# Gate units spread between the attentions of a two-layer encoder, and two softmax scalings moved to ScalarE

## The chip, the core and the metric

The kernel runs on one core of a Trainium2 chip. The metric is the device time of one execution in microseconds (us). Engines are named as in the profile: PE is TensorE, PEld its weight loads, DVE is VectorE, ACT is ScalarE, POOL is GpSimd, SP is SyncE, which here only issues transfers.

## What is computed

Two layers. Each normalises x (512 tokens of 1024), projects it to eight groups of columns, runs two kinds of attention, multiplies each by a gate, and adds an output projection to x. All data are float32.

```python
h = rmsnorm(x, norm_g[l])
proj = h @ w_in[l]                       # q_a k_a v_a g_a | q_b k_b v_b g_b
out_a = neighborhood_attention(q_a, k_a, v_a, na_rpb[l])      # group A: 8 heads of 64
out_b = diff_attention(q_b, k_b, v_b, t5_table, lam, ...)     # group B: 4 heads, two softmax maps each
y = concatenate([out_a * silu(g_a), out_b * silu(g_b)])
x = x + y @ w_out[l]
# group B: attn = softmax(map 0) - lam * softmax(map 1), then attn @ v, then an RMS norm per head
```

## The kernel before

The input projection is cut into 16 units per layer of 256 columns of w_in: `VB0 VB1` and `VA0 VA1` (values of group B and A), `QB0..QB3` and `QA0..QA3` (queries and keys of one B head, or of one pair of A heads), `GB0 GB1` and `GA0 GA1` (gates). Between them stand eight attentions, `AB0..AB3` (one B head each) and `AA0..AA3` (a pair of A heads each; below, x and y are the first and second head of a pair). The tuple `ORDER` says in which order a layer's units and attentions are written.

Every matmul is done three times for precision: each operand is split into a rounded part and the rest (`wh`, `wl`; `hTh`, `hTl`; `pth`, `ptl`). ACT makes the rounded part (line L98 for weights, L163 for results), DVE subtracts it (L101, L164). A Q or G unit is 48 matmuls of 512 columns at L210, a V unit 96 of 256 columns at L222; both write a PSUM tile `pp`, of which there are three. The output projection is L540; it starts with the halves of `y` that belong to group B.

A quarter of a B head (128 queries) is: scores on PE (L271, L272, into `st`, two buffers), DVE adds the bias and takes the minimum (L274), ACT exponentiates (L277), this for both maps; DVE takes reciprocals (L281, L282), scales the first map (L283) and subtracts the second (L284); PE transposes (L288, into `pt`, two buffers), ACT and DVE split the result (L163, L164); PE multiplies by the values (L293, into `pv`, one buffer). After a head come squares, a sum over partitions on PE (L304), DVE's `row` (L306) and on POOL three small transfers, a power (L308 to L314) and a product (L315). A quarter of an A head ("tile") is the same with 256 columns and one map: L325, L331, L334, reciprocal L336, scale L337, transposes L340, split L163/L164; after four tiles the products L347 and their sum (L353 on ACT, L354 on DVE).

A gate is evacuated by a tanh on ACT (L252) and a product on DVE (`u`, L254); POOL multiplies it into `y` (L483). `u` shares its two buffers with `rb`, which holds the norm factors of a B head.

Weights are converted two units ahead: when a unit begins, the L98 and L101 of the unit after next are written, into the buffer pair of the unit that has just begun, so they wait until PE has done with it. The program is written in `ORDER`; a list scheduler then decides, from estimates of its own, in which order each engine's queue takes the instructions. Each engine then works through its queue in that order.

Of the kernel before, what the change touches and what calls it, by code (L numbers as in the profile page):

```python
# [11 lines left out]
AF = mybir.ActivationFunctionType  # L12
# [16 lines left out]
WARM = (7, 2)  # L29
WRAW_BUFS = 2  # L30
QK_BUFS = 2
ORDER = ("VB0", "QB0", "AB0", "QB1", "VB1", "AB1", "QB2", "AB2", "QB3", "AB3", "VA0", "QA0", "AA0",
         "QA1", "AA1", "VA1", "QA2", "AA2", "QA3", "AA3", "GB0", "GB1", "GA0", "GA1")
A_TILES = ((0, 1), (1, 1), (2, 1), (0, 3))
A_SLOT = ((0, 0, 256), (1, 1, 128), (2, 1, 128), (0, 1, 768))
A_PV = ((1, 0, 128), (3, 256, 128), (0, 0, 384), (2, 128, 128))
# [5 lines left out]
def _view(t, off, dims):  # L42
    return bass.AP(tensor=t.tensor, offset=t.offset + off, ap=[list(t.ap[0])] + [list(d) for d in dims])
# [3 lines left out]
def hybrid_encoder(ctx: ExitStack, tc: tile.TileContext, x, norm_g, w_in, na_rpb,  # L47
# [18 lines left out]
    V, A, G, T = nc.vector, nc.scalar, nc.gpsimd, nc.tensor  # L66
# [95 lines left out]
    def split(ps, oh, ol):  # L162
        A.copy(out=oh, in_=ps)  # L163
        V.tensor_tensor(out=ol, in0=ps, in1=oh.bitcast(F32), op=ALU.subtract)  # L164
# [93 lines left out]
    def attn_b(h, q, k, vt, yb, nlam, sg, yout):  # L258
        pv = ps_v.tile([P, S], F32, name="pv")
        for qp in range(2):  # L260
            pth_v = w4.tile([P, 4, 256], F32R, name="pth", tag="w4k")
            ptl_v = w4.tile([P, 4, 256], F32R, name="ptl", tag="w4k")
            for qi in range(2):
                qt = 2 * qp + qi
                e = w4.tile([P, 2, S], F32, name="w4k")
                mn = small.tile([P, 2], F32, name="mn")
                z = small.tile([P, 2], F32, name="z")
                for m in range(2):
                    st = ps_s.tile([P, S], F32, name="st")
                    kh, kl = k[m]  # L270
                    T.matmul(out=st, lhsT=q[m][:, qt * P:(qt + 1) * P], rhs=kh, start=True, stop=False)  # L271
                    T.matmul(out=st, lhsT=q[m][:, qt * P:(qt + 1) * P], rhs=kl, start=False, stop=True)  # L272
                    lt = work.tile([P, S], F32, name="lt", bufs=2)
                    V.tensor_tensor_reduce(out=lt, in0=st, in1=yb[:, 48 - 16 * qt:560 - 16 * qt],  # L274
                                           scale=-1.0, scalar=3e38, op0=ALU.add, op1=ALU.min,
                                           accum_out=mn[:, m:m + 1])
                    A.activation(out=e[:, m, :].rearrange("p (b r c) -> p b r c", r=ROWS, c=C8),  # L277
                                 in_=lt.rearrange("p (r b c) -> p b r c", r=ROWS, c=C8),
                                 func=AF.Exp, bias=mn[:, m:m + 1], scale=-1.0, accum_out=z[:, m:m + 1])
                rz = small.tile([P, 2], F32, name="rz")  # L280
                V.reciprocal(out=rz, in_=z)  # L281
                V.tensor_scalar_mul(rz[:, 1:2], rz[:, 1:2], nlam)  # L282
                V.tensor_scalar_mul(e[:, 0, :], e[:, 0, :], rz[:, 0:1])  # L283
                V.scalar_tensor_tensor(out=e[:, 0, :], in0=e[:, 1, :], scalar=rz[:, 1:2], in1=e[:, 0, :],  # L284
                                       op0=ALU.mult, op1=ALU.add)
                pt = ps_t.tile([P, 4, P], F32, name="pt")
                for kt in range(4):
                    T.transpose(out=pt[:, kt, :], in_=e[:, 0, kt * P:(kt + 1) * P], identity=ident)  # L288
                split(pt, pth_v[:, :, qi * P:(qi + 1) * P], ptl_v[:, :, qi * P:(qi + 1) * P])
            n = 0  # L290
            for kt in range(4):
                for vs, pp in ((0, pth_v), (0, ptl_v), (1, pth_v)):
                    T.matmul(out=pv[:, qp * 256:(qp + 1) * 256], lhsT=vt[:, kt, h % 2, vs, :], rhs=pp[:, kt, :],  # L293
                             start=(n == 0), stop=(n == 11))
                    n += 1
        sq, su = (work.tile([64, S], F32, name=nm, tag="s2", bufs=3) for nm in ("sq", "su"))
        A.activation(out=sq, in_=pv[0:64], func=AF.Square)
        A.activation(out=su, in_=pv[64:P], func=AF.Square)
        V.tensor_tensor(out=sq, in0=sq, in1=su, op=ALU.add)
        A.activation(out=yout, in_=pv, func=AF.Copy, scale=sg)  # L300
        sr = work.tile([P, S], F32R, name="sr", tag="s2", bufs=3)
        A.copy(out=sr[0:64], in_=sq)
        V.tensor_tensor(out=sr[64:P], in0=sq, in1=sr[0:64].bitcast(F32), op=ALU.subtract)
        T.matmul(out=pv[0:2, :], lhsT=ones_r, rhs=sr, start=True, stop=True)  # L304
        row = work.tile([1, S], F32, name="row", tag="th", bufs=2)
        V.tensor_scalar(out=row, in0=pv[0:1, :], scalar1=1.0 / P, scalar2=1e-5, op0=ALU.mult, op1=ALU.add)  # L306
        ms = small.tile([P, 4], F32, name="ms")
        nc.gpsimd.dma_start(out=ms, in_=row.rearrange("o (p a) -> o p a", a=4))  # L308
        rs = small.tile([P, 4], F32, name="rsb")
        G.tensor_tensor(out=rs, in0=ms, in1=nhalf, op=ALU.pow)  # L310
        rs_d = dram.tile([1, S], F32, name="rs_d", bufs=2)
        nc.gpsimd.dma_start(out=rs_d.rearrange("o (p a) -> (o p) a", a=4), in_=rs)
        rb = work.tile([P, S], F32, name="rb", tag="u", bufs=2)
        nc.gpsimd.dma_start(out=rb, in_=rs_d.broadcast_to([P, S]))  # L314
        G.tensor_tensor(out=yout, in0=yout, in1=rb, op=ALU.mult)  # L315


    def attn_a(l, hd, half, q, k, vt, s_out):
        ba = bias_a(l, hd)
        ptt = [w4.tile([P, 4, 256], F32R, name=nm, tag="w4k") for nm in ("pth", "ptl")]  # L320
        z = small.tile([P, 4], F32, name="za")
        for j, (k0, dk) in enumerate(A_TILES):
            st = ps_s.tile([P, S], F32, name="st")
            for i in range(2):
                T.matmul(out=st[:, 0:256], lhsT=q[:, j * P:(j + 1) * P],  # L325
                         rhs=k[i].rearrange("p (t c) -> p t c", c=P)[:, k0:k0 + dk + 1:dk, :],
                         start=(i == 0), stop=(i == 1))
            e = work.tile([P, 256], F32, name="ea", bufs=3)
            mn = small.tile([P, 1], F32, name="mna")
            i0 = (0, 4, 4, 8)[j]  # L330
            V.tensor_tensor_reduce(out=e, in0=st[:, 0:256],  # L331
                                   in1=ba[:, 64 * i0:64 * i0 + 256],
                                   scale=-1.0, scalar=3e38, op0=ALU.add, op1=ALU.min, accum_out=mn)
            A.activation(out=e, in_=e, func=AF.Exp, bias=mn, scale=-1.0, accum_out=z[:, j:j + 1])  # L334
            rz = small.tile([P, 1], F32, name="rza")
            V.reciprocal(out=rz, in_=z[:, j:j + 1])  # L336
            V.tensor_scalar_mul(e, e, rz)  # L337
            pt = ps_t.tile([P, 4, P], F32, name="pt")
            for i in range(2):
                T.transpose(out=pt[:, i, :], in_=e[:, i * P:(i + 1) * P], identity=ident)  # L340
            t0, sl, stp = A_SLOT[j]
            oh, ol = (_view(p, t0 * 256 + sl * P, [[stp, 2], [1, P]]) for p in ptt)
            split(pt[:, 0:2, :], oh, ol)
        pv = ps_v.tile([P, S], F32, name="pv")
        for n, (t, q0, dq) in enumerate(A_PV):
            for i, pp in enumerate(ptt):
                T.matmul(out=_view(pv, q0, [[dq, 2], [1, P]]), lhsT=vt[:, t, hd % 4, :],  # L347
                         rhs=pp[:, t, :].rearrange("p (a b) -> p a b", b=P),
                         start=(n == 0 and i == 0), stop=(n == 3 and i == 1))
        tmp = work.tile([P, S], F32, name="tmpa", tag="s2", bufs=3)  # L350
        lo = 64 * half
        hi = 64 - lo
        A.activation(out=tmp[lo:lo + 64], in_=pv[hi:hi + 64], func=AF.Copy, scale=0.5)  # L353
        V.scalar_tensor_tensor(out=s_out[lo:lo + 64], in0=pv[lo:lo + 64], scalar=0.5, in1=tmp[lo:lo + 64],  # L354
                               op0=ALU.mult, op1=ALU.add)
# [3 lines left out]
    for l in range(DEPTH):  # L359
        seq += [(w_in[l, UNITS.index(u)], False) for u in ORDER if u in UNITS]  # L360
        seq += [(w_out[l, i], i == 3) for i in range(4)]
# [95 lines left out]
    for l in range(DEPTH):  # L457
# [38 lines left out]
        nlam, sg = lams[l]  # L496
        for n, u in enumerate(ORDER):
            kind, i = u[:2], int(u[2])
# [182 lines left out]
```

## Time and profile before

| | |
|---|---|
| median of 3 runs | 631.58 us (631.32 to 632.37) |
| the profiled execution | 631.53 us |
| its span, first to last instruction | 629.8 us |
| PE busy | 594.4 us, 94% of the span |
| DVE busy | 427.0 us, 68% |
| ACT busy | 320.2 us, 51% |
| mean granted TensorE clock | 0.977 |

The 1.7 us between time and span are outside the first and last instruction. A busy PE may still be slow: matmuls are pipelined and the table counts an engine as busy from start to modelled end. Layer 1 and 2 repeat each other with 303.4 us between them; the rows below are mostly of layer 1.

### The profile page before, as it was taken

What the parts mean: (1) busy time and instruction counts of PE and PEld (TensorE: products, weight loads), DVE (VectorE), ACT (ScalarE), POOL (GpSimd) and SP (SyncE); (2) the same over time, 40 slices, a digit from 0 to 9 for tenths busy, and PEclk for the clock granted to TensorE, in tenths of its full rate; (3) what the DMA queues carried; (4) which work ended last, traced back from release to release, by engine and by line L of the source; (5) the groups of instructions that cost most, each with busy time, mean ns of one, the idle gap of its engine ahead of it and who ended that gap; (6) DMA issues with size and microseconds to landing.
All of it is one profiled execution on the core that took longest, in us unless ns stands there. A gap on an engine that the chain in (4) does not pass through costs nothing.

```text
span 629.8 us, 9006 instructions
## 1 busy us (share of the span) xinstructions
PE 594.4 (94%) x3230; PEld 504.5 (80%) x3230; DVE 427.0 (68%) x1011; ACT 320.2 (51%) x672; POOL 73.6 (12%) x91
## 2 busy tenths in 40 slices
PE   9899995899989999999999999688998999999995
PEld 7888883788888888888898798577887888888883
DVE  2755667597887777754674576578788877777263
ACT  5433546374656555734254344635666556664232
POOL 4400000111022002200000000020101200111001
PEclk9999997989999999999999999979999999999998
DMA  6854232313533443453643533320335354226214
GB/s 233 150 187 119 86 101 85 102 47 104 139 93 117 126 137 120 137 176 132 202 134 100 163 91 99 103 68 1 85 100 143 106 154 125 93 68 206 95 67 134
DMA packets 25166, 74.48 MB, mean 118 GB/s; under 512 B 7329, under 2 KB 7329, under 8 KB 24098
## 3 DMA queue, kind: packets, MB, share of 16 engines
q1 hardware_dynamic: 23648, 71.51, 37.6%
q0 software_dynamic: 1472, 2.40, 2.3%
q8 instruction: 26, 0.43, 0.3%
q14 instruction: 18, 0.15, 0.1%
q10 hardware_dynamic: 2, 0.00, 0.0%
HBM read 60.23 MB, written 4.21 MB: 102 GB/s over the span
## 4 chain that ended last, share of the span: by engine, by line
PE 81%; DVE 10%; ACT 5%; issue 3%; POOL 0%; POOLq 0%; DVEq 0%; ACTq 0%
PE pp L210 39%; PE pp L540 11%; PE pp L222 11%; PE pv L293 3%; PE pv L347 2%; PE pt L340 2%; DVE lt L274 2%; DVE wl L101 2%; PE st L325 2%; PE st L271 2%; PE pv L540 2%; PE st L272 2%; PE pt L288 1%; PE pt L195 1%; PE pp L437 1%
## 5 line engine op out<-in xcount | busy, mean ns | idle before, releaser
L101 DVE TENSOR_TENSOR wl<-wraw,wh 128x512 fp32r<-128x512 f32 x148 | 93.5, 686 | 52.6 <-ACT wh L98 20.7
L98 ACT CAST wh<-wraw 128x1024 fp32r<-128x1024 f32 x74 | 74.3, 1048 | 67.4 <-PE pp L210 33.8
L210 PE MATMUL pp<-hTh,wl 128*128 128x512 f32 x384 | 106.1, 399 | 0.0
L210 PE MATMUL pp<-hTh,wh 128*128 128x512 f32 x384 | 102.3, 398 | 0.4 <-DVE kt L246 0.4
L210 PE MATMUL pp<-hTl,wh 128*128 128x512 f32 x384 | 102.6, 396 | 0.0
L210 PEld LDWEIGHTS pp<-hTl,wh 128*128 128x128 f32 x384 | 70.7, 188 | 14.9
L210 PEld LDWEIGHTS pp<-hTh,wh 128*128 128x128 f32 x384 | 69.7, 188 | 14.6 <-PE pt L288 0.9
L210 PEld LDWEIGHTS pp<-hTh,wl 128*128 128x128 f32 x384 | 70.1, 188 | 14.0
L163 ACT CAST pth<-pt 128x256 fp32r<-128x256 f32 (+1 forms) x96 | 42.3, 443 | 70.2 <-PE pt L288 47.5
L222 PE MATMUL pp<-wh,hTh 128*128 128x256 f32 x224 | 66.0, 295 | 7.4 <-DVE v L164 7.0
L164 DVE TENSOR_TENSOR ptl<-pt,pth 128x256 fp32r<-128x256 f32 (+1 forms) x96 | 48.6, 508 | 31.3 <-ACT pth L163 30.6
L222 PE MATMUL pp<-wh,hTl 128*128 128x256 f32 x224 | 65.4, 292 | 0.0
L222 PE MATMUL pp<-wl,hTh 128*128 128x256 f32 x224 | 65.1, 290 | 0.0
L222 PEld LDWEIGHTS pp<-wh,hTh 128*128 128x128 f32 x224 | 44.2, 197 | 10.4 <-DVE v L164 7.9
L277 ACT ACTIVATE w4k<-lt,mn 128x512 f32<-128x512 f32 x64 | 45.9, 721 | 5.4 <-DVE mn L274 5.1
L274 DVE CUSTOM_DVE_ANT_0 lt<-st,yb 128x512 f32<-128x512 f32 x64 | 43.1, 681 | 3.4 <-PE st L272 2.9
L331 DVE CUSTOM_DVE_ANT_0 ea<-st,ba 128x256 f32<-128x256 f32 x64 | 26.4, 419 | 27.3 <-PE pt L340 19.6
L222 PEld LDWEIGHTS pp<-wl,hTh 128*128 128x128 f32 x224 | 44.0, 196 | 0.6
L222 PEld LDWEIGHTS pp<-wh,hTl 128*128 128x128 f32 x224 | 43.9, 196 | 0.5
L271 PE MATMUL st<-kt,qs 128*128 128x512 f32 x64 | 29.1, 454 | 11.0 <-DVE mn L274 9.2
L483 POOL TENSOR_TENSOR y<-y,u 128x512 f32<-128x512 f32 x16 | 21.6, 1348 | 144.7 <-DVE u L254 122.2
L334 ACT ACTIVATE ea<-ea,mna 128x256 f32<-128x256 f32 x64 | 32.7, 513 | 9.7 <-DVE mna L331 8.2
(124 smaller groups left out, 1066.7 us busy)
## 6 DMA issues: line engine op xcount, KB each, us to landing
wraw<-in_w_in_dram SPq DMA_DIRECT2D x64, 512.0 KB, 4.0
kt<-kt SPq DMA_DIRECT2D x16, 512.0 KB, 4.4
wraw<-in_w_out_dram SPq DMA_DIRECT2D x16, 512.0 KB, 3.7
ba<-in_na_rpb_dram SPq DMA_DIRECT2D x16, 384.0 KB, 3.6
y<-in_x_dram SPq DMA_DIRECT2D x8, 512.0 KB, 4.5
yb<-in_t_table_dram SPq DMA_DIRECT2D x8, 280.0 KB, 2.8
rb<-rs_d POOLq DMA_DIRECT2D x8, 256.0 KB, 4.4
xs_d<-y SPq DMA_DIRECT2D x4, 512.0 KB, 4.3
```

The source lines that it names most:

```text
L98: A.copy(out=wh[:, ks, :], in_=r)
L101: V.tensor_tensor(out=wl[:, kh, :], in0=r[:, 2 * i:2 * i + 2, :], in1=wh[:, kh, :].bitcast(F32), op=ALU.subtract)
L163: A.copy(out=oh, in_=ps)
L164: V.tensor_tensor(out=ol, in0=ps, in1=oh.bitcast(F32), op=ALU.subtract)
L210: T.matmul(out=pp, lhsT=a[:, kc, cs], rhs=b[:, kc, c0:c0 + S], start=(n == 0), stop=(n == 3 * KC - 1))
L222: T.matmul(out=pp[:, 0:256], lhsT=a[kc][:, c0:c0 + P], rhs=b[:, kc, :], start=(n == 0), stop=(n == 3 * KC - 1))
L271: T.matmul(out=st, lhsT=q[m][:, qt * P:(qt + 1) * P], rhs=kh, start=True, stop=False)
L274: V.tensor_tensor_reduce(out=lt, in0=st, in1=yb[:, 48 - 16 * qt:560 - 16 * qt], scale=-1.0, scalar=3e38, op0=ALU.add, op1=ALU.min, accum_o ...
L277: A.activation(out=e[:, m, :].rearrange("p (b r c) -> p b r c", r=ROWS, c=C8), in_=lt.rearrange("p (r b c) -> p b r c", r=ROWS, c=C8), fun ...
L331: V.tensor_tensor_reduce(out=e, in0=st[:, 0:256], in1=ba[:, 64 * i0:64 * i0 + 256], scale=-1.0, scalar=3e38, op0=ALU.add, op1=ALU.min, acc ...
L334: A.activation(out=e, in_=e, func=AF.Exp, bias=mn, scale=-1.0, accum_out=z[:, j:j + 1])
L540: T.matmul(out=pp, lhsT=a[k][:, t * P:(t + 1) * P], rhs=b[:, kc, :], start=(half + kc + i == 0), stop=(half == 1 and kc == 3 and i == 2))
```

## The change

`ORDER` gets a new sequence. GB0 goes from the end of the layer to the place between QB2 and AB2, GB1 to the place before AA0, GA0 to the place before AA3; GA1 stays last. VA0 is written one attention earlier. The scaling of the first map (L283) and of group A's exponentials (L337) is written as an ACTIVATE with a per-partition scale instead of a DVE multiplication.

```diff
-ORDER = ("VB0", "QB0", "AB0", "QB1", "VB1", "AB1", "QB2", "AB2", "QB3", "AB3", "VA0", "QA0", "AA0",
-         "QA1", "AA1", "VA1", "QA2", "AA2", "QA3", "AA3", "GB0", "GB1", "GA0", "GA1")
+ORDER = ("VB0", "QB0", "AB0", "QB1", "VB1", "AB1", "QB2", "GB0", "AB2", "QB3", "VA0", "AB3", "QA0", "GB1",
+         "AA0", "QA1", "VA1", "AA1", "QA2", "AA2", "QA3", "GA0", "AA3", "GA1")
...
-                V.tensor_scalar_mul(e[:, 0, :], e[:, 0, :], rz[:, 0:1])
+                A.activation(out=e[:, 0, :], in_=e[:, 0, :], func=AF.Copy, scale=rz[:, 0:1])
...
-            V.tensor_scalar_mul(e, e, rz)
+            A.activation(out=e, in_=e, func=AF.Copy, scale=rz)
```

How the change stands in the queues, at the three places that the prediction speaks of. First DVE in layer 1 during AB1, where the last products of AB0 come in. Before, the four L101 rows convert the weights of QA0 and wait for QB3:

```order
L164 TENSOR_TENSOR ptl<-pt,pth 128x4x128
L101 TENSOR_TENSOR wl<-wraw,wh 128x512 x4
L299 TENSOR_TENSOR sq<-sq,su 64x512
L164 TENSOR_TENSOR ptl<-pt,pth 128x4x128
L274 ISA lt,mn<-st,yb 128x512
```

After the change they convert the weights of VA0 and wait for GB0, which now stands where QB3 stood:

```order
L299 TENSOR_TENSOR sq<-sq,su 64x512
L101 TENSOR_TENSOR wl<-wraw,wh 128x512 x4
L164 TENSOR_TENSOR ptl<-pt,pth 128x4x128
L303 TENSOR_TENSOR sr<-sq,sr 64x512
L274 ISA lt,mn<-st,yb 128x512
```

The four conversions stay ahead of the minimum (L274) in both; the sum of squares (L299) has moved ahead of them. Second, ACT at the start of AA0, from the evacuation of QA1's first query half (the first L231) to that of its second. Before, the values of VA1 (`v`) are evacuated between the steps of AA0:

```order
L231 ACTIVATE qs<-pp 64x512
L334 ACTIVATE ea,za<-ea,mna 128x256
L163 CAST pth<-pt 128x4x128
L163 CAST pth<-pt 128x2x128
L334 ACTIVATE ea,za<-ea,mna 128x256
L297 ACTIVATE sq<-pv 64x512
L298 ACTIVATE su<-pv 64x512
L300 ACTIVATE y<-pv,sg_366 128x512
L163 CAST v<-pp 128x4x64
L163 CAST pth<-pt 128x256
L163 CAST v<-pp 128x4x64
```

And after the change, up to just ahead of the second L231:

```order
L334 ACTIVATE ea,za<-ea,mna 128x256
L297 ACTIVATE sq<-pv 64x512
L298 ACTIVATE su<-pv 64x512
L300 ACTIVATE y<-pv,sg_366 128x512
L163 CAST pth<-pt 128x2x128
L337 ACTIVATE ea<-ea,rza 128x256
L163 CAST pth<-pt 128x256
L334 ACTIVATE ea,za<-ea,mna 128x256 x2
L302 CAST sr<-sq 64x512
L163 CAST pth<-pt 128x256
L334 ACTIVATE ea,za<-ea,mna 128x256
L337 ACTIVATE ea<-ea,rza 128x256 x2
```

The evacuations of `v` are gone from here, because VA1 comes later, and the scalings have come in. Third, PE at the end of the layer. Before, the last tiles of AA3 (L340) lie between the matmuls of the last gate unit, GA1 (L210), up to the output projection:

```order
L340 MATMUL pt<-ident,ea 128x128 x2
L210 MATMUL pp<-hTh,wh 128x512 x3
L210 MATMUL pp<-hTl,wh 128x512 x8
L210 MATMUL pp<-hTh,wl 128x512 x4
L347 MATMUL pv<-pth,v 128x256
L210 MATMUL pp<-hTh,wl 128x512
L347 MATMUL pv<-ptl,v 128x256
L210 MATMUL pp<-hTh,wl 128x512
L340 MATMUL pt<-ident,ea 128x128 x2
L210 MATMUL pp<-hTh,wl 128x512 x2
L540 MATMUL pp<-wh,yTh 128x512
```

After the change the last matmuls of GA1 are followed by most of AA3. First the rows just behind GA1:

```order
L210 MATMUL pp<-hTh,wl 128x512 x3
L347 MATMUL pv<-pth,v 128x256
L325 MATMUL st<-kt,qs 128x256 x2
L347 MATMUL pv<-ptl,v 128x256
L347 MATMUL pv<-pth,v 128x2x128
L347 MATMUL pv<-ptl,v 128x2x128
L347 MATMUL pv<-pth,v 128x256
L347 MATMUL pv<-ptl,v 128x256
L340 MATMUL pt<-ident,ea 128x128 x2
L325 MATMUL st<-kt,qs 128x256 x2
L340 MATMUL pt<-ident,ea 128x128 x2
L325 MATMUL st<-kt,qs 128x256 x2
```

From GA1's last matmul to the first L540 there stand four pairs of scores, six pairs of transposes and 14 products of values in PE's queue, and no matmul of a projection.

## Rows read from the trace of the kernel before

**Rows 1.** The page: span, and busy time by engine.
```profile
span 629.8 us, 9006 instructions
PE 594.4 (94%) x3230; PEld 504.5 (80%) x3230; DVE 427.0 (68%) x1011; ACT 320.2 (51%) x672; POOL 73.6 (12%) x91
```

**Rows 2.** Stretches: length, busy time (instructions) of each engine, clock, DMA share, GB/s.
```profile
90.00:135.00 45.00, 35.45 (x200) 29.72 (x199) 30.30 (x73) 22.74 (x48) 4.76 (x6) 0.85 0.29 77
...
165.00:195.00 30.00, 27.89 (x202) 25.41 (x201) 25.43 (x77) 20.47 (x52) 6.65 (x8) 1.00 0.42 116
...
240.00:274.00 34.00, 34.00 (x176) 28.43 (x175) 25.85 (x65) 21.72 (x47) 6.86 (x5) 1.00 0.44 138
...
390.00:437.00 47.00, 37.09 (x209) 30.55 (x209) 32.55 (x77) 23.25 (x49) 4.07 (x5) 0.89 0.28 78
```

**Rows 3.** Timeline of DVE: start, us, instruction, [idle before <-releaser].
```profile
97.61 2.50 DVE L101 TENSOR_TENSOR wl<-wraw,wh 128x512 fp32r<-128x512 f32 x4 [6.79 <-ACT sq L297]
...
100.62 0.68 DVE L164 TENSOR_TENSOR ptl<-pt,pth 128x512 fp32r<-128x512 f32 x1
101.22 0.67 DVE L274 CUSTOM_DVE_ANT_0 lt<-st,yb 128x512 f32<-128x512 f32 x1
```

**Rows 4.** Timeline of PE from 96 to 114 us.
```profile
96.56 0.95 PE L210 MATMUL pp<-hTh,wl 128*128 128x512 f32 x3
101.96 0.50 PE L271 MATMUL st<-kt,qs 128*128 128x512 f32 x1 [4.45 <-DVE mn L274]
...
110.22 0.41 PE L222 MATMUL pp<-wh,hTh 128*128 128x256 f32 x1
...
112.78 0.33 PE L222 MATMUL pp<-wh,hTh 128*128 128x256 f32 x1
```

**Rows 5.** Stretches again: the two holes of 90 to 135 us.
```profile
97.50:110.20 12.70, 5.78 (x15) 3.25 (x15) 12.37 (x28) 7.82 (x17) 1.14 (x2) 0.70 0.34 105
...
118.00:127.00 9.00, 6.37 (x39) 4.88 (x38) 6.30 (x18) 4.81 (x12) 1.28 (x1) 0.97 0.09 33
```

**Rows 6.** Groups by line and shape: count | busy us, mean ns of one | idle before.
```profile
L277 ACT ACTIVATE w4k<-lt,mn 128x512 f32<-128x512 f32 x64 | 45.9, 721 | 5.4 <-DVE mn L274 5.1
...
L334 ACT ACTIVATE ea<-ea,mna 128x256 f32<-128x256 f32 x64 | 32.7, 513 | 9.7 <-DVE mna L331 8.2
...
L337 DVE TENSOR_SCALAR ea<-ea,rza 128x256 f32<-128x256 f32 x64 | 25.7, 402 | 1.4
...
L163 ACT CAST pth<-pt 128x256 fp32r<-128x256 f32 x64 | 23.8, 372 | 22.5 <-PE pt L340 22.0
...
L231 ACT ACTIVATE qs<-pp 64x512 fp32r<-64x512 f32 x32 | 19.0, 593 | 28.9 <-DVE qs L232 13.7 <-PE st L325 8.7 <-PE pp L210 4.4
...
L283 DVE TENSOR_SCALAR w4k<-w4k,rz 128x512 f32<-128x512 f32 x32 | 16.1, 504 | 0.0
...
L163 ACT CAST yTh<-y 128x512 fp32r<-128x512 f32 x16 | 9.5, 617 | 5.4 <-POOL y L483 5.4
...
L300 ACT ACTIVATE y<-pv,sg 128x512 f32<-128x512 f32 x8 | 5.5, 688 | 0.2
...
L574 ACT ACTIVATE xn<-xn,rs 128x384 f32<-128x384 f32 x4 | 2.5, 617 | 3.7 <-POOL rs L169 3.7
```

**Rows 7.** Timeline of PE at the end of layer 1.
```profile
264.14 2.03 PE L210 MATMUL pp<-hTl,wh 128*128 128x512 f32 x8
266.00 2.03 PE L210 MATMUL pp<-hTh,wl 128*128 128x512 f32 x8
...
274.14 0.39 PE L540 MATMUL pp<-wh,yTh 128*128 128x512 f32 x1
```

**Rows 8.** Timeline of POOL after AB1's `row`.
```profile
133.57 0.57 POOL L308 DMA_DIRECT2D ms<-row  x1 [12.81 <-DVE row L306]
...
139.43 0.54 POOL L314 DMA_DIRECT2D rb<-rs_d  x1 [1.87 <-DMA rs_d<-rsb]
144.11 1.58 POOL L315 TENSOR_TENSOR y<-y,rb 128x512 f32<-128x512 f32 x1 [4.14 <-DMA rb<-rs_d]
```

## The prediction

> **What bounds the kernel now.** The page comes first [rows 1]: PE is busy 594.4 us of a span of 629.8, DVE 427.0, ACT 320.2. Time can change in two ways: PE's 35 us without work shrink or grow, or PE's matmuls run slower. So I next read the stretches [rows 2] and compare length with PE's busy time. At the end of the layer (240 to 274 us), where four gate units run beside the last attention, PE works 34.00 of 34.00 us. From 90 to 135 us it works 35.45 of 45.00 at a granted clock of 0.85 (a mean over its two levels, 1.2 and 2.4 GHz, as every such share here), and in the same place of layer 2 (390 to 437) 37.09 of 47.00 at 0.89. From 165 to 195, where AA0 begins, 2.11 of 30 are idle. Most of what PE loses is thus in the B attentions; the gates now lie where nothing is lost.
>
> Why is PE idle at 97? DVE's timeline [rows 3]: the conversion of a weight unit (four L101, 2.50 us) stands ahead of a minimum (L274, 0.67 us). It waits until PE is done with the unit whose buffers it takes, DVE is idle 6.79 us, and PE, which has run out of projection work, waits 4.45 us for that minimum [rows 4]. PE's last L210 there begin at 96.56; the next projection matmul is the L222 at 110.22. The three L210 off, the hole is some 13.0 us long, and the 15 matmuls of the attention in it [rows 5] are worth about 2.5 us at the price below. A second hole, 118 to 127, has 6.37 us of work in 9.00 [rows 5].
>
> One price for all that follows: eight 512-column matmuls start in 266.00 - 264.14 = 1.86 us, 0.2325 each [rows 7]; one of 256 columns is taken as half, 0.116. Just after the hole twelve 256-column matmuls take 112.78 - 110.22 = 2.56 us, 0.213 each [rows 4], in a stretch whose granted clock is 0.70 [rows 5]: the cost of coming out of a hole is 12 x (0.213 - 0.116) = 1.16 us.
>
> **The scalings.** They leave DVE: 32 x 0.504 (L283) and 64 x 0.402 (L337), 16.1 + 25.7 = 41.8 us [rows 6], so DVE falls to some 385. The trace has no such scaling on ACT in these shapes. For 128x512 the nearest rows lie between L574's 0.617 (the same form, 384 columns) and L277's 0.721; I take 0.70, by L300's 0.688, which has the form and the width. For 128x256 they lie between L163's 0.372 (a copy) and L334's 0.513 (an exponential); I take 0.51, since a pointer is read in both. That is 32 x 0.70 + 64 x 0.51 = 55 us on ACT (43.5 to 55.9 by the bounds), from 320 to 375, 60% of the span. Neither engine is near full, so this is worth nothing directly. On a chain, a B quarter gets 0.2 us longer and an A tile 0.11, a handoff between engines aside. What hides that is projection work on PE; where it is missing, the scaling counts, and there I put it into the sums below.
>
> A rule speaks against this half of the change: the Trainium skill, "ScalarE: Activation LUTs", section "Rules for kernel authors", says to put plain multiplications on VectorE. These rows agree in direction: 0.504 and 0.402 on DVE are below the exponentials of the same width on ACT. The same page, section "What ACT_TABLE_LOAD costs", would price a scaling with one pointer at 0.71 and 0.49 us (my estimates from its 186 ns, 93 ns and 0.833 ns per element), 54 us in all, so the sum would not move.
>
> **GB0 and VA0 in the B attentions.** The plan puts a gate's 48 matmuls into the stretch with the holes. But the queues show where they go: ahead of the hole, not into it. DVE still has four L101 ahead of the minimum; they are now VA0's and wait for GB0's last matmul, as QA0's waited for QB3's. After GB0, PE has no projection work until QB3, which waits as VA0 did. So the first hole stays as long: from L101's start to the next projection matmul it was 110.22 - 97.61 = 12.6 us [rows 3, 4], and I keep that. What PE can do in it grows: one sum (L304), four maps of scores (8 matmuls of 512 columns), two sets of transposes (0.23 each) and 12 products: 9 x 0.2325 + 2 x 0.23 + 12 x 0.116 = 3.95. Lost 12.6 - 3.95 = 8.65, against 13.0 - 2.5 = 10.5: -1.9.
>
> The second hole comes between QB3's two halves: the two gate tiles hold two of the three `pp`, so QB3's second half needs the first half's tile evacuated. On ACT that evacuation stands behind L297, L298 and L300 of AB1, which wait for AB1's last products, which wait for its last transposes, which stand behind QB3's first half. The chain: transposes 0.23, L163 0.617, L164 0.68, products 1.4, three ACT steps 0.593 + 0.593 + 0.688, then L231 0.593, an exponential 0.721, L163 0.617, L302 0.593, L231 0.593, DVE's half of the evacuation 0.68: 8.6 us, and the transposes and scores ahead of the products 1.2: 9.8 [rows 3, 6] (where a step has no row, one of the same size stands for it). PE has 4.2 us of work in that time, 5.6 are lost; the hole there now loses 9.00 - 6.37 = 2.63 [rows 5]: +3.0. Together **+1.1 us** per layer. Were the first hole cut to 2 us lost, it would be 2 - 10.5 + 3.0 = -5.5; with no work at all in the second, 1.1 + 4.2 = +5.3.
>
> `u` and `rb` share two buffers, so L254 for GB0's second half waits until POOL has multiplied the first into `y` (L483), which stands behind L308 to L314 and L315 of a B head. From L308's start to L314's end that took 139.43 + 0.54 - 133.57 = 6.4 us [rows 8], and a gate product follows: some 7.7 us in which DVE stands, with the next minima and L101 behind it. I cost it at nothing, since QB3's second half and three quarters of VA0 give PE 24 x 0.2325 + 72 x 0.116 = 13.9 us there; without that cover it is up to 7.7 us, twice per layer.
>
> **GB1 and AA0.** After GB1 the only projection work is QA1's first half, 24 x 0.2325 = 5.6 us. Its second half waits for the second query half's evacuation, and from the first L231 to it ACT has 16 instructions: two L231 and L297, L298, L302 at 0.593, four L334 at 0.513, L300 at 0.688, three L163 at 0.372, three L337 at 0.51: 8.35 us, then DVE 0.68: 9.0 [rows 3, 6]. PE has 23 matmuls of 256 columns, eight of 128 and a sum meanwhile, 3.4 us; 5.6 are lost, against 2.1 there now [rows 2]: **+3.5** (0 if the evacuation is served early, 6 with the slower matmuls after a hole).
>
> **GA1 and AA3.** Now AA3's last tiles are hidden below GA0 and GA1, and L540 follows L210 without a gap: eight L210 from 266.00, L540 at 274.14 [rows 7]. After the change, when GA1 ends, ACT still has 17 instructions ahead of the first split of `y` (L163, yTh): five L334, five L337, five L163, a tanh and an L353 (0.617 at most each): 5 x (0.513 + 0.51 + 0.372) + 1.23 = 8.2, then the split 0.617, and about 1 because the next minimum stands behind the four L101 of 2.50 us: 9.8 to L540 [rows 3, 6]. PE has four pairs of scores, six pairs of transposes, 14 products: (8 + 6 + 14) x 0.116 = 3.25. Lost 6.55, and 1.16 for the slow matmuls behind it: **+7.7** (5 to 10).
>
> **Sum.** 1.1 + 3.5 + 7.7 = 12.3 per layer, 24.6 for two. From the profiled execution's 631.5 (span 629.8 and 1.7 around it; the median of the runs, 631.58, is the same) that is **656 us**.
>
> **The rivals.** (a) Faster: the gates do fill the holes and the tail is covered. Then the idle time of the two B stretches, 9.55 + 9.91 = 19.5 us [rows 2], goes: 612 us. It needs VA0's L101 to be through before PE runs dry (a first hole below about 4 us) and ACT's lead over GA1 larger than the queue says. For it: PE works every microsecond where gates and an attention lie side by side. Against: the L101 stands ahead of the minimum as before, and both ends of the layer lose their cover. (b) The gains in the B stretches pay for the tail: -5.5 instead of +1.1 gives 631.5 + 2 x 5.7 = 643, with the early evacuation in AA0 636, with the lower bound of the tail too 631; 628 to 641 as a range. (c) The buffers of `u` stop DVE without cover: 7.7 more per layer, 671 us; it decides if L254's wait for L483 lasts longer than those 13.9 us. For it: rows 8 show how slow that list on POOL is. (d) ACT becomes what PE waits for in general, as the rule above would have it: the 32 tiles of AA1 and AA2 in both layers would lose 0.11 each and as much again in handoffs, some 7 us: 663. That is inside the forecast's range.
>
> **How the numbers follow.** Forecast, with (d): 0.70, its own range 641 to 668. (a) 0.12, (b) 0.10, (c) 0.08. The predicted time is the forecast's. A range of 634 to 674 leaves out (a), a third of (b) and a little of (c), some 0.17. About 0.2% (1.3 us) is what a measurement can tell from no change. Faster holds (a) and a third of (b): 0.15; same 0.04; slower 0.81.
>
> **What would show it.** Right: in front of each layer's first L540 an idle time of several us with ACT's yTh (or what precedes it) as releaser, and a granted clock below 1 near 265 to 285 us, where it is 1.00 now; an idle PE before QA1's second half; a hole around 97 to 110 that stays, with DVE idle in front of VA0's L101; ACT near 375, DVE near 385. Wrong: L210 running into L540 as before, or the stretch from 90 to 135 with PE above 95% busy. For (c): L254 idle for over 7 us behind POOL's L483, with PE idle at the same time.

## The result, and the profile after

The changed kernel takes 657.45 us (657.06 to 658.53, four runs) against 631.45 us; the ratio is 1.0409, 95% interval 1.0381 to 1.0438. The forecast was 656. In the profiled execution the span grows from 629.8 to 656.7 us and the mean granted clock falls from 0.977 to 0.962. The page of the changed kernel, lines as in [rows 1]:

```profile
span 656.7 us, 8995 instructions
PE 607.6 (93%) x3230; PEld 511.1 (78%) x3230; DVE 398.0 (61%) x915; ACT 366.9 (56%) x768; POOL 74.1 (11%) x91
```

DVE has lost 29 us and ACT has gained 47 (the forecast had DVE near 385 and ACT near 375), both are near 60%, and the time went up all the same. The two scalings, grouped by line and shape (count | busy us, mean ns of one | idle before):

```profile
L337 ACT ACTIVATE ea<-ea,rza 128x256 f32<-128x256 f32 x64 | 31.6, 507 | 8.6 <-DVE rza L336 8.6
L283 ACT ACTIVATE w4k<-w4k,rz 128x512 f32<-128x512 f32 x32 | 22.9, 717 | 9.3 <-DVE rz L281 9.2
```

So the prices are 0.507 and 0.717 us, where 0.51 and 0.70 were taken. The estimates from the Trainium skill, "ScalarE: Activation LUTs", section "What ACT_TABLE_LOAD costs", were 0.49 and 0.71; the trace agrees with them.

Now the four places of the forecast. PE's timeline of the changed kernel in layer 1; each pair of rows is the last projection matmuls ahead of a hole (a row with x8 starts eight of them) and the first behind it:

```profile
95.75 1.65 PE L210 MATMUL pp<-hTh,wl 128*128 128x512 f32 x6
101.63 0.40 PE L304 MATMUL pv<-sr,ones_r 128*2 128x512 f32 x1 [4.23 <-DVE sr L303]
...
110.55 2.03 PE L210 MATMUL pp<-hTh,wh 128*128 128x512 f32 x8
...
116.38 0.86 PE L210 MATMUL pp<-hTh,wl 128*128 128x512 f32 x3
...
126.97 0.59 PE L304 MATMUL pv<-sr,ones_r 128*2 128x512 f32 x1 [3.57 <-DVE sr L303]
127.69 3.78 PE L210 MATMUL pp<-hTh,wh 128*128 128x512 f32 x8
131.27 2.73 PE L210 MATMUL pp<-hTl,wh 128*128 128x512 f32 x8
133.84 1.09 PE L210 MATMUL pp<-hTh,wl 128*128 128x512 f32 x4
...
188.45 0.86 PE L210 MATMUL pp<-hTh,wl 128*128 128x512 f32 x3
...
198.49 3.29 PE L210 MATMUL pp<-hTh,wh 128*128 128x512 f32 x8 [0.49 <-DVE qs L232]
201.62 0.63 PE L210 MATMUL pp<-hTl,wh 128*128 128x512 f32 x2
...
274.89 0.95 PE L210 MATMUL pp<-hTh,wl 128*128 128x512 f32 x3
...
285.21 0.80 PE L540 MATMUL pp<-wh,yTh 128*128 128x512 f32 x1 [0.20 <-ACT yTh L163]
```

With 0.2325 us for each L210 of the first row of a pair, the holes last 110.55 - 97.15 = 13.4 us, 127.69 - 117.08 = 10.6, 198.49 - 189.15 = 9.3 and 285.21 - 275.59 = 9.6. The forecast had 13.0 for the first as it was before (12.6 from L101's start, below), and 9.8, 9.0 and 9.8 for the others. Layer 2 has the same four: 14.3 us up to 430.10, 10.6 up to 447.22, 9.3 up to 516.18 and 9.5 up to 603.95. The stretches themselves (length, then busy time of PE, its loads, DVE, ACT and POOL, granted clock, DMA share, GB/s):

```profile
97.50:110.50 13.00, 7.53 (x29) 5.58 (x30) 12.11 (x27) 8.91 (x20) 2.71 (x4) 0.74 0.37 103
117.10:127.70 10.60, 5.95 (x35) 4.02 (x33) 8.65 (x23) 9.65 (x20) 0.00 (x0) 0.92 0.10 26
189.00:198.50 9.50, 6.35 (x39) 4.41 (x37) 7.19 (x23) 8.37 (x22) 0.57 (x1) 0.96 0.15 43
275.00:285.20 10.20, 6.86 (x39) 5.16 (x37) 8.17 (x27) 8.44 (x25) 1.28 (x1) 0.89 0.51 149
```

The last line answers to the end of the layer in [rows 2, 7], where nothing was lost. Note how little such a hole shows as idle time: PE is called busy for 6.86 of 10.20 us with 39 short matmuls whose work is 3 to 4 us. The idle time is in small pieces, and a busy share does not show a late chain. Adding matmuls at their price and comparing with the length does; below, what a place "loses" is its length less that work.

DVE's timeline at the first hole answers to [rows 3]:

```profile
97.17 0.68 DVE L299 TENSOR_TENSOR sq<-sq,su 64x512 f32<-64x512 f32 x1 [6.65 <-ACT su L298]
97.78 2.48 DVE L101 TENSOR_TENSOR wl<-wraw,wh 128x512 fp32r<-128x512 f32 x4
100.18 0.67 DVE L164 TENSOR_TENSOR ptl<-pt,pth 128x512 fp32r<-128x512 f32 x1
100.89 0.68 DVE L303 TENSOR_TENSOR sr<-sq,sr 64x512 fp32r<-64x512 f32 x1
101.61 0.69 DVE L274 CUSTOM_DVE_ANT_0 lt<-st,yb 128x512 f32<-128x512 f32 x1
```

The four L101 still stand ahead of the minimum. DVE's 6.65 us without work now lie in front of L299, which stands just ahead of them, and end with ACT's squares of AB0 (L298). From the start of the L101 to the next projection matmul it is 110.55 - 97.78 = 12.8 us, where 12.6 was kept from before.

### The profile page after: what moved, and what is told of

The parts are those of the page before. It is cut to its first block, busy times and chain, and to the rows that moved or that the text cites. A ratio compares the mean times of both kernels' runs of the same rounds, so it can differ in the third digit from the quotient of the medians.

```text
span 656.7 us, 8995 instructions
## 1 busy us (share of the span) xinstructions
PE 607.6 (93%) x3230; PEld 511.1 (78%) x3230; DVE 398.0 (61%) x915; ACT 366.9 (56%) x768; POOL 74.1 (11%) x91
## 4 chain that ended last, share of the span: by engine, by line
PE 69%; DVE 16%; ACT 6%; issue 4%; DMA 3%; POOL 1%; POOLq 0%; DVEq 0%; ACTq 0%; SPq 0%
PE pp L210 36%; PE pp L222 8%; PE pp L540 7%; DVE wl L101 5%; PE pv L293 3%; PE st L271 2%; PE pv L347 2%; PE st L325 2%; PE st L272 2%; PE pt L340 1%; PE pt L288 1%; DVE ptl L164 1%; DVE lt L274 1%; PE pv L540 1%; ACT wh L98 1%
## 5 line engine op out<-in xcount | busy, mean ns | idle before, releaser
L101 DVE TENSOR_TENSOR wl<-wraw,wh 128x512 fp32r<-128x512 f32 x148 | 100.3, 734 | 43.0 <-PE pp L210 23.6
L210 PE MATMUL pp<-hTh,wh 128*128 128x512 f32 x384 | 105.8, 415 | 1.6 <-DVE qs L232 1.1
L210 PE MATMUL pp<-hTl,wh 128*128 128x512 f32 x384 | 105.0, 402 | 0.0
L210 PE MATMUL pp<-hTh,wl 128*128 128x512 f32 x384 | 104.0, 398 | 0.0
L210 PEld LDWEIGHTS pp<-hTh,wh 128*128 128x128 f32 x384 | 74.6, 199 | 19.2 <-DVE qs L232 2.7
L210 PEld LDWEIGHTS pp<-hTl,wh 128*128 128x128 f32 x384 | 73.2, 192 | 16.4 <-issue 0.2
L210 PEld LDWEIGHTS pp<-hTh,wl 128*128 128x128 f32 x384 | 70.4, 188 | 14.7
L222 PE MATMUL pp<-wh,hTh 128*128 128x256 f32 x224 | 63.4, 283 | 2.1 <-DVE v L164 1.9
L222 PE MATMUL pp<-wh,hTl 128*128 128x256 f32 x224 | 63.8, 285 | 0.0
L222 PE MATMUL pp<-wl,hTh 128*128 128x256 f32 x224 | 63.1, 282 | 0.0
L274 DVE CUSTOM_DVE_ANT_0 lt<-st,yb 128x512 f32<-128x512 f32 x64 | 43.4, 682 | 10.9 <-PE st L272 10.1
L222 PEld LDWEIGHTS pp<-wh,hTh 128*128 128x128 f32 x224 | 42.2, 188 | 4.2 <-DVE v L164 2.5
L222 PEld LDWEIGHTS pp<-wl,hTh 128*128 128x128 f32 x224 | 42.2, 188 | 0.4
L222 PEld LDWEIGHTS pp<-wh,hTl 128*128 128x128 f32 x224 | 42.2, 188 | 0.3
L483 POOL TENSOR_TENSOR y<-y,u 128x512 f32<-128x512 f32 x16 | 21.7, 1354 | 168.9 <-DVE u L254 91.3
L337 ACT ACTIVATE ea<-ea,rza 128x256 f32<-128x256 f32 x64 | 31.6, 507 | 8.6 <-DVE rza L336 8.6
```

The source lines that it names most:

```text
L101: V.tensor_tensor(out=wl[:, kh, :], in0=r[:, 2 * i:2 * i + 2, :], in1=wh[:, kh, :].bitcast(F32), op=ALU.subtract)
L210: T.matmul(out=pp, lhsT=a[:, kc, cs], rhs=b[:, kc, c0:c0 + S], start=(n == 0), stop=(n == 3 * KC - 1))
L222: T.matmul(out=pp[:, 0:256], lhsT=a[kc][:, c0:c0 + P], rhs=b[:, kc, :], start=(n == 0), stop=(n == 3 * KC - 1))
L337: A.activation(out=e, in_=e, func=AF.Copy, scale=rz)
```

## Experiments

Each ratio is against the kernel before on the same chip (medians 632.7, 632.4 and 633.7 us in the three sets). Every new order lets the list scheduler lay out all queues again, so an edit is never quite alone.

**The halves of the change.** e1_scal has the scalings only:

```diff
-                V.tensor_scalar_mul(e[:, 0, :], e[:, 0, :], rz[:, 0:1])
+                A.activation(out=e[:, 0, :], in_=e[:, 0, :], func=AF.Copy, scale=rz[:, 0:1])
...
-            V.tensor_scalar_mul(e, e, rz)
+            A.activation(out=e, in_=e, func=AF.Copy, scale=rz)
```

> Order of before, both scalings on ACT. Theory (the order of the units costs the time, the scalings lie beside PE's projection work): 631 to 635 us. Rival (ACT becomes what PE waits for): 640 us or more, with ACT as the releaser of most of PE's new idle time.

Measured: 630.2 us, ratio 0.9954 (0.9923 to 0.9984): a little faster, just below the range of the theory. The rival is out: ACT is at 58%, and PE's waits that end with ACT add up to 0.9 us.

e2_order has the new `ORDER` only, the scalings stay on DVE.

> New order, scalings on DVE as before. Theory: 652 to 657 us, since the three losses (B stretch, AA0, end of layer) come from the order; at the end of the layer ACT's list is 5 x 0.51 us shorter and DVE's 5 x 0.40 longer, so L540 may start 1 us earlier per layer. Rival (the scalings on ACT make the loss): below 645 us.

Measured: 680.06 us, ratio 1.0765 (1.0699 to 1.0831). Both expectations fail: the order costs 47 us by itself, and the scalings give back 23 of them. They are worth 2.5 us in the old order and 22.6 in the new one.

**Which scaling.** n_l283 is the changed kernel with L337 back on DVE, n_l337 with L283 back on DVE.

> The changed kernel with L337 (group A's scaling) back on DVE, L283 (the first map's) on ACT. Theory (in the new order PE waits for DVE's list in every stretch without projection work, so each scaling counts where it stands; the A stretches lost 7 to 8 us more with the scalings on DVE than in the changed kernel): 662 to 668 us. Rival (the 22 us between both scalings on DVE and both on ACT come from L283 and L337 together only, or from another plan of the queues): 657 or less, or 673 or more.

> The changed kernel with L283 back on DVE, L337 on ACT. Theory (as for the other half; the B stretches lost some 15 us more with the scalings on DVE): 669 to 676 us. Rival: 662 or less.

Measured: 658.41 us (1.0419, 1.0369 to 1.0468), between the two ranges named, and 676.82 us (1.0708, 1.0653 to 1.0762), 0.8 above the range of the theory. The edit of L283 alone gives all of it; L337's place makes no difference that can be told from none (657.45 against 658.41). The second hole shows a part. PE's timeline of e2_order, scaling on DVE:

```profile
116.78 0.39 PE L210 MATMUL pp<-hTh,wl 128*128 128x512 f32 x1
...
127.95 1.09 PE L288 MATMUL pt<-ident,w4k 128*128 128x128 f32 x4 [1.14 <-DVE w4k L284]
131.28 0.59 PE L304 MATMUL pv<-sr,ones_r 128*2 128x512 f32 x1 [2.24 <-DVE sr L303]
132.73 3.78 PE L210 MATMUL pp<-hTh,wh 128*128 128x512 f32 x8 [0.86 <-DVE qs L232]
```

and of n_l283, scaling on ACT:

```profile
115.97 0.86 PE L210 MATMUL pp<-hTh,wl 128*128 128x512 f32 x3
...
126.56 0.59 PE L304 MATMUL pv<-sr,ones_r 128*2 128x512 f32 x1 [3.56 <-DVE sr L303]
127.29 3.78 PE L210 MATMUL pp<-hTh,wh 128*128 128x512 f32 x8
```

The hole lasts 132.73 - 117.0 = 15.7 us in the one and 127.29 - 116.7 = 10.6 in the other, and in the first PE waits again and again for DVE's minima and products. It also holds two pairs of score matmuls more, 0.9 us, so 4.2 us more are lost, of some 11 per layer between the two runs.

How much of this is the time that DVE spends on the scaling, and how much is the other layout of the queues? Other traces answer most of it. In e7_wlpool, an experiment below, both scalings are on ACT, and PE's rows in this hole are those of e2_order, one for one:

```profile
114.73 1.56 PE L212 MATMUL pp<-hTh,wl 128*128 128x512 f32 x6
...
130.52 3.78 PE L212 MATMUL pp<-hTh,wh 128*128 128x512 f32 x8
```

That is 14.4 us, 1.3 less than in e2_order. In n_l337 the scaling is on DVE in both layers; the hole lasts 15.7 us in layer 1 with e2_order's rows, and in layer 2, where the queue is nearly that of the changed kernel, 457.80 - 446.4 = 11.4. So in the second hole the scaling itself is worth about 1 us per layer, and the rest of the difference comes with the layout. A second place says the same. Behind QA1 e2_order has a hole that the changed kernel and n_l283 do not have, with four L101 ahead of the split that PE waits for; it loses 3.7 us in each layer (here DVE's row, then PE's two):

```profile
211.09 2.50 DVE L101 TENSOR_TENSOR wl<-wraw,wh 128x512 fp32r<-128x512 f32 x4 [0.52 <-ACT th L252]
214.07 0.41 PE L340 MATMUL pt<-ident,ea 128*128 128x128 f32 x2 [2.12 <-DVE ptl L164]
216.55 0.57 PE L222 MATMUL pp<-wh,hTh 128*128 128x256 f32 x1
```

No scaling stands on DVE there. The same hole is in e7_wlpool (up to 215.79), in f_gb1 (up to 192.38) and in e4_va0back (up to 214.21), all with the scalings on ACT, and loses some 4 us per layer. The 22 us are thus what the edit of L283 does to the program, and for the larger part not what DVE's half microsecond does. Why the scheduler's layout changes with it was not found out.

**GA0 behind AA3 again.** e3_gaend:

```diff
-         "AA0", "QA1", "VA1", "AA1", "QA2", "AA2", "QA3", "GA0", "AA3", "GA1")
+         "AA0", "QA1", "VA1", "AA1", "QA2", "AA2", "QA3", "AA3", "GA0", "GA1")
```

> The changed kernel with GA0 written after AA3 again, ahead of GA1. Theory: the 22 us of the two gate units cover AA3's last tiles, L540 follows L210 without a gap and the term of the tail (7.0 to 7.7 us per layer) goes: 642 to 645 us. Rival (AA3's tail is long whatever stands behind it, or AA3's start loses as much without GA0): 652 us or more.

Measured: 657.9 us, ratio 1.0399 (1.0351 to 1.0447). This is no test of either: PE, ACT, DVE and POOL get exactly the queues of the changed kernel. The scheduler draws GA0 ahead of AA3's late tiles from both places. GA0's new place is thus no cause of anything; at the end of the layer two gate units are left because GB0 and GB1 are gone.

**One unit at a time**, from e1_scal: f_gb0 moves GB0 alone to its new place, f_gb1 moves GB1 alone, f_va0 moves VA0 alone, f_gb0va0 moves GB0 and VA0. e4_va0back is the changed kernel with VA0 behind AB3 again, which leaves GB0 and GB1 moved (and GA0, which by e3_gaend changes nothing). The edit of f_gb0 as the pattern:

```diff
-ORDER = ("VB0", "QB0", "AB0", "QB1", "VB1", "AB1", "QB2", "AB2", "QB3", "AB3", "VA0", "QA0", "AA0",
-         "QA1", "AA1", "VA1", "QA2", "AA2", "QA3", "AA3", "GB0", "GB1", "GA0", "GA1")
+ORDER = ("VB0", "QB0", "AB0", "QB1", "VB1", "AB1", "QB2", "GB0", "AB2", "QB3", "AB3", "VA0", "QA0",
+         "AA0", "QA1", "AA1", "VA1", "QA2", "AA2", "QA3", "AA3", "GB1", "GA0", "GA1")
```

> Order of before with GB0 alone moved to QB2, scalings on ACT. Theory (GB0 does not fill the hole, it moves it; three gate units are left as cover at the end and AA3's last products come behind them): B attentions within 3 us per layer of before, 2 us per layer lost at the end, 633 to 641 us. Rival (GB0 fills the holes and the loss of the whole change lies in the other moves): 625 us or less.

> Order of before with GB1 alone moved ahead of AA0, scalings on ACT. Theory (AA0 loses 3.5 to 5 us per layer, because only QA1's first half lies beside it after GB1; the end loses 2): 639 to 646 us. Rival (AA0 keeps its time, the loss there needs VA0 or GB0 moved too): 630 to 635 us.

> Order of before with VA0 alone one attention earlier, scalings on ACT. Theory (no cover is lost anywhere, VA0's products only lie one attention earlier): 627 to 634 us. Rival (the early VA0 costs, or pays for a part): outside of these bounds by over 3 us.

> The changed kernel with GB1 at the end again: GB0 and VA0 moved, scalings on ACT. Theory (VA0 is worth something only where a gate has made a hole: behind GB0 it fills 6 to 8 us in AB2 and AB3 that GB0 alone loses): 639 to 645 us, against 649.0 with GB0 alone. Rival (VA0 is worth nothing here either, as it was by itself): 647 to 651 us.

> The changed kernel with VA0 behind AB3 again. Theory: the two holes of the B attentions come from GB0 (its conversion's place and the PSUM tiles it holds), not from VA0, so within 4 us of the changed kernel: 653 to 661 us. Rival (VA0 written one attention earlier makes them): 650 us or less.

Measured, all with the scalings on ACT:

| moved | us | ratio (95%) | against e1_scal |
|---|---|---|---|
| nothing (e1_scal) | 630.2 | 0.9954 (0.9923 to 0.9984) | |
| VA0 (f_va0) | 630.05 | 0.9956 (0.9922 to 0.9990) | -0.2 |
| GB0 (f_gb0) | 649.01 | 1.0276 (1.0219 to 1.0333) | +18.8 |
| GB0, VA0 (f_gb0va0) | 643.06 | 1.0166 (1.0108 to 1.0223) | +12.9 |
| GB1 (f_gb1) | 656.57 | 1.0373 (1.0308 to 1.0437) | +26.4 |
| GB0, GB1 (e4_va0back) | 671.41 | 1.0599 (1.0539 to 1.0659) | +41.2 |
| all | 657.45 | 1.0409 (1.0381 to 1.0438) | +27.2 |

Each of the two gates that leave the end costs 9 to 13 us per layer, and the two nearly add up (45 against 41). VA0 is worth nothing by itself, 6 us beside GB0 and 14 beside both gates (e4_va0back's runs spread from 669.3 to 678.4 us). f_va0 and f_gb0va0 came out inside the ranges of their theories; f_gb0, f_gb1 and e4_va0back came out 8 to 11 us above theirs.

The places in the traces say which unit makes which hole. GB0 alone makes the second one: it lasts 10.6 us in f_gb0 (up to 127.27) as in the changed kernel, and 5.9 in e1_scal. GB1 alone makes AA0's: 9.1 us in f_gb1 (up to 178.70), and 6.5 before. What the expectation of f_gb1 lacked is mainly the hole behind QA1 shown above, and so it is with e4_va0back, whose second hole is 10.6 us in layer 1, with VA0 behind AB3: as expected, VA0 does not make it. VA0 does not fill it either: it lasts 10.6 us in f_gb0va0 too. So f_gb0va0 met its number but not its reason; of the 14 us beside both gates some 8 go with the hole behind QA1, and where the other gains of VA0 lie was not found out. The end of the layer in f_gb0, with three gate units left (PE's waits: us in all, times, longest):

```profile
PE pp L540 <- ACT yTh L163: 3.5, 2, 1.8
```

PE does wait there for the split of `y`, 1.8 us in each layer, even with three units as cover; some 2 us were expected.

**The wait for POOL.** In the changed kernel DVE's timeline after AB1's `row` reads

```profile
129.06 0.67 DVE L254 SCALAR_TENSOR_TENSOR u<-th,pp 128x512 f32<-128x512 f32 x1
137.09 0.69 DVE L254 SCALAR_TENSOR_TENSOR u<-th,pp 128x512 f32<-128x512 f32 x1 [7.36 <-POOL y L483]
137.69 0.68 DVE L164 TENSOR_TENSOR ptl<-pt,pth 128x512 fp32r<-128x512 f32 x1
138.30 4.67 DVE L101 TENSOR_TENSOR wl<-wraw,wh 128x512 fp32r<-128x512 f32 x4
```

as the forecast had it: 7.36 us for some 7.7. n_ubuf gives `rb` a buffer of its own:

```diff
-        rb = work.tile([P, S], F32, name="rb", tag="u", bufs=2)
+        rb = work.tile([P, S], F32, name="rb", tag="rb", bufs=1)
```

> The changed kernel with a buffer of its own for rb, so that L254 does not wait for POOL's L483. Theory (the 7.4 us that DVE stands there lie beside QB3's second half and VA0 on PE): the wait goes and the time stays, 654 to 659 us. Rival (the standing DVE is what AB3 and VA0 wait for afterwards): 650 us or less.

Measured: 660.28 us, ratio 1.0446 (1.0394 to 1.0498), no better than the changed kernel and 1.3 above the range of the theory. DVE's timeline of n_ubuf:

```profile
130.04 0.69 DVE L254 SCALAR_TENSOR_TENSOR u<-th,pp 128x512 f32<-128x512 f32 x1 [0.66 <-ACT th L252]
137.02 0.69 DVE L164 TENSOR_TENSOR ptl<-pt,pth 128x512 fp32r<-128x512 f32 x1 [6.29 <-ACT pth L163]
```

The wait for POOL is gone and DVE stands as long for the next thing, AB2's transposes, which lie behind QB3's second half on PE. The wait was not quite free: from VA0's first matmul to QA0's first, layer 1 of the changed kernel takes 16.5 us (137.57 to 154.03) and that of n_ubuf 14.9 (137.13 to 152.07), both with 13.7 us of work. n_ubuf loses more than that elsewhere, so its total does not show this.

**The four L101 off DVE.** e7_wlpool lets POOL compute them for VA0's weights:

```diff
-                V.tensor_tensor(out=wl[:, kh, :], in0=r[:, 2 * i:2 * i + 2, :], in1=wh[:, kh, :].bitcast(F32),
+                L.tensor_tensor(out=wl[:, kh, :], in0=r[:, 2 * i:2 * i + 2, :], in1=wh[:, kh, :].bitcast(F32),
```

(`L` is POOL for this unit, DVE for all others.)

> The changed kernel with the rest of VA0's weights (L101, the four that stand ahead of the minimum in the first hole) computed on POOL instead of DVE. Theory (the first hole is made by these 2.5 us on DVE and what queues behind them): the first hole shrinks by 2.5 to 4 us per layer, 649 to 653 us. Rival (PE there waits for ACT's or its own chain, not for DVE's list): within 2 us of the changed kernel.

Measured: 674.14 us, ratio 1.0673 (1.0612 to 1.0733): neither in the total. PE's and POOL's timelines of e7_wlpool (two lines were added, so its L306 is the other kernels' L304):

```profile
95.38 1.65 PE L212 MATMUL pp<-hTh,wl 128*128 128x512 f32 x6
100.44 0.59 PE L306 MATMUL pv<-sr,ones_r 128*2 128x512 f32 x1 [3.41 <-DVE sr L305]
...
107.33 3.36 PE L212 MATMUL pp<-hTh,wh 128*128 128x512 f32 x8
```

```profile
97.17 5.59 POOL L103 TENSOR_TENSOR wl<-wraw,wh 128x512 fp32r<-128x512 f32 x4 [72.85 <-PE pp L212]
```

At the place itself the theory holds: the hole lasts 107.33 - 96.8 = 10.5 us instead of 13.4, though the queue puts fewer matmuls into it (13 instead of 29), so that the loss falls by 1.2 us only, from 9.4 to 8.1. PE's wait falls from 4.23 to 3.41 us, POOL needs 5.59 us for what DVE did in 2.48, and the rest of the layer is laid out worse: the second hole lasts 14.4 us instead of 10.6, and the one behind QA1 is there. What the four L101 cost in the total, the run does not decide.

## Why the prediction was right

**The first hole stays.** 12.8 us from L101's start, 12.6 forecast, and PE has the work counted: right. GB0 went ahead of the hole, not into it. Two readings were loose. The forecast has L101 wait for PE; [rows 3] name ACT's square (L297) as the releaser, and PE's last L210 ends 0.10 us before L101 starts, so that the rows fit either. And it sets 12.6 us after the change against 13.0 before; from PE's last projection matmul on both sides it is 13.4 against 13.0, and the gain is 1.1 us, not 1.9.

**The second hole** is 10.6 us instead of 9.8. What the sum left out is the clock behind it: the eight L210 from 127.69 take 3.58 us and the next eight 2.57, against 1.86 each, 2.4 us in a stretch that starts at the lower of the two levels (granted clock 0.50 from 127.70 to 131.20):

```profile
127.70:131.20 3.50, 3.50 (x8) 2.79 (x9) 2.00 (x3) 0.00 (x0) 0.57 (x1) 0.50 0.06 7
```

Before, the fifteen L222 from 126.56 on came at some 0.21 us each instead of 0.116, 1.4 us, so about 1 us of this is new, and it is in no term.

**AA0.** 9.3 us to QA1's second half, with DVE's qs (L232) as the releaser: forecast 9.0, right. The eight L210 behind it take 201.62 - 198.49 = 3.13 us, 1.3 too many, which the forecast had put into its bound, not into its value.

**The end of the layer.** L540 begins 9.6 us after GA1's last matmul, forecast 9.8, with ACT's yTh as the last releaser. Wrong was the sign to look for: there is no idle time of several us ahead of L540, but pieces between AA3's matmuls. The 1.16 us for slow matmuls behind it came in layer 1 (granted clock 0.87 from 285.2 to 290.0) and not in layer 2 (1.00 from 604.0 to 609.0).

**The sum came out better than its terms.** The forecast charged its two sides by different rules. What the changed kernel loses is length less work at the price; what the kernel before loses in the second hole and at AA0 is PE's idle time, 2.63 and 2.11 us, and that is too little, as idle time is above. PE's timeline of the kernel before, the last projection matmul ahead of each of the two places and the first behind it:

```profile
118.74 0.29 PE L222 MATMUL pp<-wh,hTl 128*128 128x256 f32 x1
...
126.56 0.58 PE L222 MATMUL pp<-wh,hTh 128*128 128x256 f32 x1 [2.35 <-DVE v L164]
...
175.58 0.28 PE L222 MATMUL pp<-wh,hTl 128*128 128x256 f32 x1
...
182.23 0.39 PE L222 MATMUL pp<-wh,hTh 128*128 128x256 f32 x1 [1.13 <-DVE v L164]
```

The first is 126.56 - 118.86 = 7.7 us long with eight matmuls of 512 columns, twelve of 256 and eight of 128, 3.7 us: 4.0 are lost. The second is 6.5 us long with 2.9 of work: 3.6 are lost. With one rule on both sides (us per layer; two values are layer 1 and 2):

| place | lost before | lost after | more | forecast |
|---|---|---|---|---|
| first hole | 10.4 | 9.4, 10.4 | -1.1, 0 | -1.9 |
| second hole | 4.0, 4.6 | 6.4 | +2.4, +1.8 | +3.0 |
| AA0 | 3.6 | 5.6 | +2.0 | +3.5 |
| end of the layer | 0 | 6.3 | +6.3 | +6.55, and 1.16 behind it |

The four places give 9.8 us per layer, against 12.3 forecast, and the two executions differ by 13.5 per layer in their spans. Some 3.7 us per layer thus lie where the forecast put nothing: in slow matmuls behind the holes, and in small waits such as PE's for a transfer of `kt` at 151.70, 1.16 us; they are not all accounted for. The direction, the four places and the size at the end of the layer were right. That 656 lies within 1.5 us of 657.45 is partly luck: two terms that were too large made up for what was left out.

**The wait for POOL** was all but hidden, as costed; by n_ubuf at most some 1.5 us per layer were at stake.

**The scalings: a wrong step with no effect on the total.** "This is worth nothing directly" holds in the old order, where the move is worth 2.5 us. In the new order the edit of L283 is worth some 20 us, for the larger part through the layout of the queues. The total did not suffer, because the lengths of the holes were counted from the queues of the changed kernel, with the scalings already on ACT. A forecast of the order alone by the same sums, 652 to 657 us for e2_order, missed 680 by far. One scaling of the first map is 0.717 us on ACT against 0.504 on DVE. The rule of the Trainium skill, "ScalarE: Activation LUTs", section "Rules for kernel authors", to use VectorE for plain multiplications, agrees with that price. Which kernel is faster it does not tell: that is the one with the scaling on ACT in both orders (658.4 against 680.1 us in the new one, most of it by the layout; in the old one 630.2 against 632.7, with L337 moved too).

**What was not foreseen** is how much a move costs away from its own place. The forecast's places belong to the units that it named, as the single moves show. But GB0 alone costs 9.4 us per layer and GB1 alone 13, where the sums at their places give less, and the two together with VA0 cost hardly more than GB1 alone: losses move from place to place when another unit is moved.

e1_scal is faster than the kernel before by 0.5% (0.2 to 0.8%); f_va0 does the same.

## What to carry to other kernels

Count what a place loses as the length between two projection matmuls less the work between them at its price, from the queues of the changed program; the busy share hides it. Work that can be done at any time is worth most where the longest chain of short steps ends, so count what is left there before any of it is spent elsewhere. Charge the kernel before by the same rule as the kernel after; else the difference is between two rules. Measure both halves of a change apart and together, and where a small edit is worth far more than the instructions it touches, compare the queues row by row before the gain is put down to an engine: here most of it was another layout.

## What the runs showed of the hardware

The four L101 that take 2.48 us at 97.78 take 4.67 us at 138.30, with the same shapes. POOL's timeline of the changed kernel at that time:

```profile
139.13 1.59 POOL L315 TENSOR_TENSOR y<-y,rb 128x512 f32<-128x512 f32 x1 [2.08 <-DMA rb<-rs_d]
140.80 1.62 POOL L483 TENSOR_TENSOR y<-y,u 128x512 f32<-128x512 f32 x1
```

The four L101 are not alike. Read one by one, the two that begin before the first product take 0.68 us each, and the other two 1.78 and 1.77; the last of them, and a product with nothing of DVE beside it:

```profile
141.20 1.77 DVE L101 TENSOR_TENSOR wl<-wraw,wh 128x512 fp32r<-128x512 f32 x1
```

```profile
135.76 1.30 POOL L483 TENSOR_TENSOR y<-y,u 128x512 f32<-128x512 f32 x1
```

Both slow ones began while a product ran and ended 0.55 us after it (140.80 + 1.62 = 142.42, and 141.20 + 1.77 = 142.97), and the two products beside them took 1.59 and 1.62 us instead of 1.30. In the whole execution seven L101 began while L315 or L483 ran; they took 1.59 to 1.78 us and each ended 0.55 us after the product. Every other L101 took at most 0.69. Over the whole kernel the mean of an L101 is 0.734 us, against 0.685 in e1_scal. No run here took POOL's products away alone. The Trainium skill, "SBUF — State Buffer", section "Who interferes with whom", says that a VectorE instruction with two inputs in SBUF contends with a GpSimd instruction that reads SBUF; L101 is one with two such inputs, and these rows agree.
